# Moving the A products of a chunked delta-rule recurrence out of its per-chunk chain

## The chip, the cores and the metric

The kernel runs on one core of one Trainium2 chip. The metric is the device time of one execution in microseconds (us); lower is better. Five engines work side by side, each in the fixed order of its own instruction stream: TensorE (PE in the profile; its weight loads are PEld), VectorE (DVE), ScalarE (ACT), GpSimd (POOL), and SyncE (SP), which here only issues transfers. PSUM is the memory that PE writes its products to; SBUF holds everything else on the core.

## The reference

A decoder block over 2048 positions of 1024 channels. The input is normalised and modulated, then one projection `p = h @ w_in` feeds two branches: a causal depthwise convolution of width 31 with a layer norm, and an RWKV-7 time mixer. Both are gated, projected, merged and projected once more; the result is added to the residual and normalised. The part that matters here is the recurrence of the mixer, per head of 64 channels (16 heads):

```python
def step(state, inp):
    r_t, w_t, k_t, v_t, kk_t, b_t = inp
    sk = jnp.einsum('bhvk,bhk->bhv', state, kk_t)
    state = (state * w_t[:, :, None, :] - sk[..., None] * b_t[:, :, None, :]
             + v_t[..., None] * k_t[:, :, None, :])
    return state, jnp.einsum('bhvk,bhk->bhv', state, r_t)
```

After it, `o` gets a normalisation per head (the groupnorm below), a bonus term `r*k*v`, and the gate. All of it is in 32-bit floating point.

## The kernel before

**Tiling.** The sequence is cut into 4 blocks of 512 positions (`TB`), the 16 heads into 4 groups of 4 heads, and a group into two pairs `q`; a pair fills 128 partitions with two heads `hh`. So `group` runs 16 times. Inside a block the recurrence goes over 8 chunks `c` of 64 positions (`CH`, `NCH`). With chunks, the recurrence becomes matrix products: a 64x64 matrix per chunk and head that says how positions of the chunk act on each other, its triangular inverse, and one state `S` (per group and pair 128x128, block diagonal) that is handed from chunk to chunk.

**One group.** `pair` is a generator in three parts for each pair: it computes decays and projects and shifts k, r and v (`shifted`), fills `KR` (k and r for a chunk side by side) and `BK`, multiplies them into the matrices `As` (L513 to L531, with `BKz` as a copy of `BK` whose other head's rows are zero), puts v into its half of `uv` (L539), and transposes `BK` into `tk`. `As` of one chunk holds four 64x64 quarters: an even chunk (`e` = 0) has the inverse's quarter in partitions 64 to 127 (`prow`, `kcol`) and v in partitions 0 to 63 of `uv` (`vrow`, `rcol`); an odd chunk the other way round. Then the inverse is made: the diagonal 32x32 blocks go through memory to POOL, which inverts them by 31 steps (L589), and come back; two rounds of 32x32 products on PE (L623, L632) in the PSUM tile `late` fill the quarters between.

**The chain.** L654 to L694 go over the 8 chunks. For each one: ACT scales the state (`Se`); PE multiplies `KR` with the state into `xo` (L665); PE adds the A·v products to it, four products over 64 rows of `As` and `uv` (L670); DVE copies the x half of `xo` to `X` (L673); PE multiplies the inverse with `X` (L679); DVE scales into the other half of `uv` (L681); PE multiplies `tk` with `uv` (L685); DVE makes the new state (L690). The output of the chunk before is finished in between: `olast` adds o's A products (L650, four products over all 128 rows) to the r half of the same `xo`, and ACT copies it to `O`, which lies in `uv`. Behind the last chunk stand the groupnorm on DVE, POOL and ACT (L707 to L716), transposes of `O` on PE into `late` (L721), and the store.

**Around it.** While a chain waits, PE works on projections (`mm3`, L192): those of the convolution, of the gates, and of the next group's pairs. Each f32 value there is split in two parts, high and low, and three products are made. The convolution's 31 taps run on DVE (L756). Behind the last group, the block outputs are projected (phase 2, from L901 on), with loads through the buffers `ld` (L917) for the mixer's output of the next block (`osplit`). Phase 2's buffers on the left side of SBUF open when those of the groups close (`late.close()`, L967), so after the last group's transposes.

**What sets the order.** The program is written in the order above, and a planner with a model of the engines' times (`schedule_with_timeline_sim=True`) writes each engine's instruction stream: of what is ready in its model, what stands first in the program goes first. Each tag of a pool has a fixed number of buffers (`bufs`), and a new tile waits until a buffer is free; `late` has one PSUM bank, `aux` and `xo` two each. Between engines, semaphores do the waiting.

Of the kernel before, what the change touches and what calls it, by code (L numbers as in the profile page):

```python
# [39 lines left out]
VVT, SHT, RKT, RHT, YT = "r", "sh", "k", "sh", "y"  # L40
# [42 lines left out]
def hybrid_block(ctx: ExitStack, tc: tile.TileContext, x, vecs, convk, w2a2, final_g, ada, w_in, w_co, w_ro, w_o, crow, out,  # L83
# [359 lines left out]
    def pair(b, q_, pr, h, lora, uv, Asb, rn, res):  # L443
# [69 lines left out]
        for hh in range(2):  # L513
            hs = slice(64 * hh, 64 * hh + 64)
            nc.scalar.copy(BKz[hs, hh], BK[hs])
        for c4 in range(NCH // 4):
            for hh in range(2):
                pA = pa.tile([P, 2, 256], F32, name="aux", tag="aux")
                for c in range(4):
                    cc, e = (c4 * 4 + c) // 2, c % 2  # L520
                    es = slice(e * 128, e * 128 + 128)
                    nc.tensor.matmul(pA[:, c // 2, es], BKz[:, hh, cc, es], KR[:, cc, es],  # L522
# [35 lines left out]
    def group(b, g, h, lora, fill):  # L558
# [8 lines left out]


# [71 lines left out]
        O = uv[:, 0::2]  # L640
        Sg = S[g]
        prev = None

        def olast(c, xo):

            vr, rc = vrow(c % 2), rcol(c % 2)
            for q in range(2):
                for hh in range(2):
                    hs = slice(64 * hh, 64 * hh + 64)
                    nc.tensor.matmul(xo[vr, q, hs], As[q][:, hh, c, rc], uv[:, c, q, hs],  # L650
                                     start=False, stop=(q == 1 and hh == 1), skip_group_check=True)
            nc.scalar.copy(O[vr, c // 2], xo[vr, 0:2])  # L652

        for c in range(NCH):  # L654
            cc, e = c // 2, c % 2
            pr_, vr = prow(e), vrow(e)
# [4 lines left out]


            xo = px.tile([P, 4, P], F32, name="xo", tag="xo")
            for q in range(2):
                nc.tensor.matmul(xo[:, q, :], R[q]["KR"][:, cc, es], Sg[:, q, :], start=(q == 0), stop=False,  # L665
                                 skip_group_check=True)
            for q in range(2):
                for hh in range(2):
                    hs = slice(64 * hh, 64 * hh + 64)
                    nc.tensor.matmul(xo[pr_, q, hs], As[q][vr, hh, c, kcol(e)], uv[vr, c, q, hs],  # L670
                                     start=False, stop=False, skip_group_check=True)
            X = lt.tile([P, 2, P], F32, name="X", tag="X", bufs=1)
            nc.vector.tensor_copy(X[pr_], xo[pr_, 0:2])  # L673
            if prev:
                olast(*prev)
            for q in range(2):
                for hh in range(2):
                    hs = slice(64 * hh, 64 * hh + 64)
                    nc.tensor.matmul(xo[pr_, q, hs], As[q][pr_, hh, c, kcol(e)], X[pr_, q, hs],  # L679
                                     start=(q == 0 and hh == 0), stop=(q == 1 and hh == 1), skip_group_check=True)  # L680
# [3 lines left out]
            for q in range(2):  # L684
                nc.tensor.matmul(xo[:, 2 + q, :], R[q]["tk"][:, c, :], uv[:, c, q, :], start=False, stop=(q == 1),  # L685
                                 skip_group_check=True)
            for q in range(2):
                for hh in range(2):
                    hs = slice(64 * hh, 64 * hh + 64)
                    nc.vector.scalar_tensor_tensor(out=Sg[hs, q, hs], in0=xo[hs, 2 + q, hs],  # L690
                                                   scalar=R[q]["pe"][hs, c:c + 1], in1=Se[hs, q, hs],
                                                   op0=ALU.mult, op1=ALU.add)
            prev = (c, xo)
        olast(*prev)  # L694


# [437 lines left out]
```

## Time and profile before

| | |
|---|---|
| median of 3 runs | 3144.74 us (3140.74 to 3146.39) |
| span of the profiled execution, first to last instruction | 3131.2 us |
| mean granted TensorE clock | 0.981 |
| busy, share of the span: PE, PEld | 96%, 90% |
| busy: DVE, POOL, ACT | 69%, 36%, 33% |
| matmul instructions | 25672 |

The profile shows one execution. The median of the runs is 13.5 us above its span, for what lies before the first and after the last instruction and for the difference between runs; the profiled execution has no time of its own beside the span. Rows of the profile read: line of the code, engine, operation, output<-input, shape, count | busy us, mean ns of one | us for which the engine sat idle just before, and for what. Rows of the timeline read: start us, length us, engine, line, operation, output<-input, shape, count. A matmul of f32 values is two instructions. "Busy" joins overlapping instructions, so the sum of single durations is larger than the busy time.

### The profile page before, as it was taken

To read this page: it belongs to the slowest core of one execution; us is meant where nothing else is said; L and a number is where in the kernel's file an instruction comes from. 1 tells how busy PE (TensorE), PEld (TensorE's weight loads), DVE (VectorE), ACT (ScalarE), POOL (GpSimd) and SP (SyncE) were. 2 spreads that over 40 slices of the span, in tenths; PEclk is the share of its full clock that TensorE was granted. 3 is DMA by queue.
4 is the path that set the end of the run, shared out by engine and by line. 5 is a ranking of instruction groups with operands and counts; after the bars stand their busy time and mean duration, and the time that the engine had idled before them with its cause. 6 is when DMAs were issued, how large, how long until landed. Compare 5 with 4: busy or idle time off the path is not lost.

```text
span 3131.2 us, 64840 instructions
## 1 busy us (share of the span) xinstructions
PE 2990.4 (96%) x25672; PEld 2808.5 (90%) x25672; DVE 2169.9 (69%) x4326; ACT 1045.9 (33%) x1887; POOL 1125.1 (36%) x1692
## 2 busy tenths in 40 slices
PE   6799998999999999999999999999999999699998
PEld 5789998999999999999999999999999988487888
DVE  6686877676767665867667586758598455977643
ACT  4424333333323242423142324132332223343421
POOL 3354545424342424141313235326256014643100
PEclk9899999999999999999999999999999999899999
DMA  8665758563747476545546557636457657756554
GB/s 300 215 240 191 259 199 275 195 235 126 256 141 244 150 244 216 190 156 182 178 164 194 186 193 243 198 130 214 137 166 262 215 174 264 261 198 232 189 185 158
DMA packets 343328, 638.42 MB, mean 204 GB/s; under 512 B 133424, under 2 KB 152176, under 8 KB 343024
## 3 DMA queue, kind: packets, MB, share of 16 engines
q1 hardware_dynamic: 343024, 634.27, 60.4%
q8 instruction: 202, 3.31, 0.4%
q14 instruction: 102, 0.84, 0.1%
HBM read 462.10 MB, written 170.92 MB: 202 GB/s over the span
## 4 chain that ended last, share of the span: by engine, by line
PE 71%; DVE 10%; DMA 9%; POOL 4%; issue 2%; SPq 2%; ACT 2%; DVEq 0%; POOLq 0%; ACTq 0%
PE ps_main L192 50%; PE aux L522 3%; PE xo L679 2%; PE xo L650 2%; PE xo L670 2%; DMA w_st<-w_in_t 2%; PE xo L665 2%; PE xo L685 2%; PE pout L1055 1%; POOL TT L593 1%; PE pout L1056 1%; PE pout L1054 1%; POOL itmp L591 1%; DVE acc L756 1%; DMA w_gr<-grow_d 1%
## 5 line engine op out<-in xcount | busy, mean ns | idle before, releaser
L192 PE MATMUL ps_main<-h_hi,w_hi 128*128 128x256 f32 x4608 | 954.9, 285 | 23.1 <-ACT w_hi L175 19.7
L192 PE MATMUL ps_main<-h_hi,w_lo 128*128 128x256 f32 x4608 | 959.1, 285 | 8.1 <-POOL w_lo L177 6.6
L192 PE MATMUL ps_main<-h_lo,w_hi 128*128 128x256 f32 x4608 | 959.0, 285 | 0.0
L192 PEld LDWEIGHTS ps_main<-h_hi,w_hi 128*128 128x128 f32 x4608 | 718.8, 190 | 33.6 <-ACT w_hi L175 20.8
L192 PEld LDWEIGHTS ps_main<-h_hi,w_lo 128*128 128x128 f32 x4608 | 717.2, 189 | 17.9 <-POOL w_lo L177 8.2
L192 PEld LDWEIGHTS ps_main<-h_lo,w_hi 128*128 128x128 f32 x4608 | 717.7, 189 | 6.8 <-issue 0.5
L756 DVE SCALAR_TENSOR_TENSOR acc<-u,ck,acc 128x512 f32<-128x512 f32 x928 | 697.9, 752 | 20.4
L175 ACT CAST w_hi<-w_st 128x1024 fp32r<-128x1024 f32 x135 | 141.5, 1048 | 327.7 <-DMA w_st<-w_in_t 120.8
L591 POOL TENSOR_TENSOR itmp<-La,TT 128x126 f32<-128x126 f32 (+22 forms) x496 | 179.8, 363 | 137.4 <-DMA La<-dA 102.1
L690 DVE SCALAR_TENSOR_TENSOR S<-xo,pe,Se 64x64 f32<-64x64 f32 x512 | 144.8, 283 | 108.4 <-PE xo L685 99.1
L593 POOL TENSOR_TENSOR TT<-TT,itmp 128x126 f32<-128x126 f32 (+22 forms) x496 | 191.9, 387 | 36.0
L177 DVE TENSOR_TENSOR w_lo<-w_st,w_hi 128x1024 fp32r<-128x1024 f32 x88 | 117.8, 1339 | 110.0 <-PE ps_main L192 53.7
L660 ACT ACTIVATE Se<-S,pe 128x128 f32<-128x128 f32 x256 | 89.1, 394 | 232.7 <-DVE S L690 232.3
L177 POOL TENSOR_TENSOR w_lo<-w_st,w_hi 128x1024 fp32r<-128x1024 f32 x47 | 112.5, 2394 | 136.2 <-ACT w_hi L175 83.5
L545 POOL TENSOR_TENSOR vv<-rk,vv 128x512 f32<-128x512 f32 x32 | 43.2, 1350 | 324.4 <-ACT rk L544 324.4
L681 DVE TENSOR_TENSOR uv<-xo,rn 64x256 f32<-64x256 f32 x128 | 53.9, 421 | 129.7 <-PE xo L679 128.7
L522 PE MATMUL aux<-KR,BKz 128*128 128x128 f32 x1024 | 139.9, 282 | 2.8 <-DVE As L524 2.1
L522 PEld LDWEIGHTS aux<-KR,BKz 128*128 128x128 f32 x1024 | 126.2, 194 | 5.7 <-DVE As L524 2.4
L524 DVE TENSOR_TENSOR As<-aux,maskA 128x512 f32<-128x512 f32 x128 | 86.8, 687 | 52.8 <-PE aux L522 51.9
L673 DVE COPY X<-xo 64x256 f32<-64x256 f32 x128 | 53.6, 419 | 89.5 <-PE xo L670 88.6
L652 ACT COPY uv<-xo 64x256 f32<-64x256 f32 x128 | 46.8, 365 | 175.7 <-PE xo L650 175.2
L665 PE MATMUL xo<-S,KR 128*128 128x128 f32 x512 | 96.4, 280 | 6.9 <-DVE S L690 6.7
(294 smaller groups left out, 5464.1 us busy)
## 6 DMA issues: line engine op xcount, KB each, us to landing
w_hi<-kh_in SPq DMA_DIRECT2D x219, 512.0 KB, 3.8
w_lo<-kl_in SPq DMA_DIRECT2D x219, 512.0 KB, 4.9
w_st<-w_in_t SPq DMA_DIRECT2D x73, 512.0 KB, 4.4
kh_in<-w_hi SPq DMA_DIRECT2D x71, 512.0 KB, 2.9
kl_in<-w_lo SPq DMA_DIRECT2D x71, 512.0 KB, 4.3
w_st<-w_ro_t SPq DMA_DIRECT2D x32, 512.0 KB, 3.9
w_st<-w_co_t SPq DMA_DIRECT2D x32, 512.0 KB, 3.5
w_hi<-kh_o SPq DMA_DIRECT2D x32, 512.0 KB, 3.6
```

The source lines that it names most:

```text
L175: nc.scalar.copy(hi, st)
L177: lo_eng.tensor_tensor(out=lo, in0=st, in1=hi.bitcast(F32), op=ALU.subtract)
L192: nc.tensor.matmul(ps[:, qs], ww[:, k, :], aa[k][:, qs], start=(k == 0 and t == 0 and q == 0), stop=(k == KT - 1 and t == 2 and q == ms - ...
L522: nc.tensor.matmul(pA[:, c // 2, es], BKz[:, hh, cc, es], KR[:, cc, es], start=(c == 0), stop=(c == 3), skip_group_check=True)
L524: nc.vector.tensor_tensor(out=Asb[:, hh, c4 * 4:c4 * 4 + 4, :].rearrange("p (a e) n -> p a (e n)", e=2), in0=pA, in1=flat(maskA).unsqueeze ...
L591: nc.gpsimd.tensor_tensor(out=tmp[:, :ni, :nt], in0=La[:, j:j + 1, j + 1:].broadcast_to([P, ni, nt]), in1=TT[:, :ni, j:j + 1].broadcast_to ...
L593: nc.gpsimd.tensor_tensor(out=TT[:, :ni, j + 1:], in0=TT[:, :ni, j + 1:], in1=tmp[:, :ni, :nt], op=ALU.add)
L650: nc.tensor.matmul(xo[vr, q, hs], As[q][:, hh, c, rc], uv[:, c, q, hs], start=False, stop=(q == 1 and hh == 1), skip_group_check=True)
L660: nc.scalar.mul(Se[:, q, :], Sg[:, q, :], R[q]["pe"][:, c:c + 1])
L665: nc.tensor.matmul(xo[:, q, :], R[q]["KR"][:, cc, es], Sg[:, q, :], start=(q == 0), stop=False, skip_group_check=True)
L690: nc.vector.scalar_tensor_tensor(out=Sg[hs, q, hs], in0=xo[hs, 2 + q, hs], scalar=R[q]["pe"][hs, c:c + 1], in1=Se[hs, q, hs], op0=ALU.mult ...
L756: nc.vector.scalar_tensor_tensor(out=acc if i + 1 < HALO else yj, in0=u[:, i:i + TB], scalar=ck[:, j, i:i + 1], in1=acc, op0=ALU.mult, op1 ...
```

## The change

- **A·v ahead of the inverse.** A new tile `XO` (8 chunks, both pairs, 128 partitions, one buffer) is set to zero in the `vrow` rows by POOL, two memsets a group. For four chunks at a time, sixteen A·v products (the same as L670's) go into one PSUM tile of the tag `aux`, and ACT copies it to `XO`, two copies each time.
- **The chain.** L670, the copy to `X` and `olast` go. DVE adds `XO[:, c]` to both halves of `xo` in place, over 128 partitions; the inverse's products read `XO`.
- **o behind the last state.** For four chunks at a time, o's sixteen A products go into one PSUM tile of the tag `late`. They are held behind the last of the chain's `tk` products in PE's stream (`issue_after`). DVE adds them into `XO`, two adds each time, and `O` now is a view of `XO`.
- **Room for XO.** `BKz` holds four chunks, not eight, and is filled twice (ACT, four half copies a pair for two whole ones); `y` shares the buffer of `M`, `s_lo` that of `sq`; `ld` in phase 2 has five buffers for six.

```diff
-VVT, SHT, RKT, RHT, YT = "r", "sh", "k", "sh", "y"
+VVT, SHT, RKT, RHT, YT = "r", "sh", "k", "sh", "M"
...
-        lo = e1.tile([P, TB], F32R, name="s_lo", tag="s_lo")
+        lo = e1.tile([P, TB], F32R, name="s_lo", tag="sq")
...
-    BKz = c1.tile([P, 2, NCH // 2, 4 * CH], F32, name="BKz")
+    BKz = c1.tile([P, 2, NCH // 4, 4 * CH], F32, name="BKz")
...
-        for hh in range(2):
-            hs = slice(64 * hh, 64 * hh + 64)
-            nc.scalar.copy(BKz[hs, hh], BK[hs])
         for c4 in range(NCH // 4):
+            for hh in range(2):
+                hs = slice(64 * hh, 64 * hh + 64)
+                nc.scalar.copy(BKz[hs, hh], BK[hs, c4 * 2:c4 * 2 + 2])
...
+        XO = lt.tile([P, NCH, 2, P], F32, name="XO", tag="XO", bufs=1)
+        for e in range(2):
+            nc.gpsimd.memset(XO[vrow(e), e::2], 0.0)
+        heads = [(q, hh) for q in range(2) for hh in range(2)]
+        for c4 in range(NCH // 4):
+            pv = pa.tile([P, 2, 2, P], F32, name="aux", tag="aux")
+            for c in range(4 * c4, 4 * c4 + 4):
+                e = c % 2
+                for q, hh in heads:
+                    hs = slice(64 * hh, 64 * hh + 64)
+                    nc.tensor.matmul(pv[prow(e), c // 2 % 2, q, hs], As[q][vrow(e), hh, c, kcol(e)], uv[vrow(e), c, q, hs],
...
+            for e in range(2):
+                nc.scalar.copy(XO[prow(e), 4 * c4 + e:4 * c4 + 4:2], pv[prow(e)])
...
-            for q in range(2):
-                for hh in range(2):
-                    hs = slice(64 * hh, 64 * hh + 64)
-                    nc.tensor.matmul(xo[pr_, q, hs], As[q][vr, hh, c, kcol(e)], uv[vr, c, q, hs],
-                                     start=False, stop=False, skip_group_check=True)
-            X = lt.tile([P, 2, P], F32, name="X", tag="X", bufs=1)
-            nc.vector.tensor_copy(X[pr_], xo[pr_, 0:2])
-            if prev:
-                olast(*prev)
...
+            nc.vector.tensor_tensor(out=XO[:, c], in0=xo[:, 0:2], in1=XO[:, c], op=ALU.add)
...
+        O = XO[:, 0::2]
+        for c4 in range(NCH // 4):
+            po = pl.tile([P, 2, 2, P], F32, name="late", tag="late")
+            with tc.issue_after(last.ins if hasattr(last, "ins") else last):
+                for c in range(4 * c4, 4 * c4 + 4):
+                    e = c % 2
+                    for q, hh in heads:
+                        hs = slice(64 * hh, 64 * hh + 64)
+                        nc.tensor.matmul(po[vrow(e), c // 2 % 2, q, hs], As[q][:, hh, c, rcol(e)], uv[:, c, q, hs],
...
+            for e in range(2):
+                sl = slice(4 * c4 + e, 4 * c4 + 4, 2)
+                nc.vector.tensor_tensor(out=O[vrow(e), 2 * c4:2 * c4 + 2], in0=po[vrow(e)], in1=XO[vrow(e), sl], op=ALU.add)
...
-        t_ = ob.tile([P, TB], F32, name=name, tag="ld", bufs=6)
+        t_ = ob.tile([P, TB], F32, name=name, tag="ld", bufs=5)
```

More of the change, by code (lines that the diff above doesn't have):

```diff
@@ L521, in pair @@
                     es = slice(e * 128, e * 128 + 128)
-                    nc.tensor.matmul(pA[:, c // 2, es], BKz[:, hh, cc, es], KR[:, cc, es],
+                    nc.tensor.matmul(pA[:, c // 2, es], BKz[:, hh, c // 2, es], KR[:, cc, es],
                                      start=(c == 0), stop=(c == 3), skip_group_check=True)
@@ L637, in group @@
                 nc.vector.tensor_copy(As[q][lo_, :, e::2, hi_], pq[lo_, q])
[L640 removed]
         Sg = S[g]
[L642 to L652 removed]
         for c in range(NCH):
             cc, e = c // 2, c % 2
[L656 removed]
+            pr_ = prow(e)
             es = slice(e * 128, e * 128 + 128)
```

35 lines of the change are left out of this document (16 added, 19 removed).

## The prediction

> **What bounds the kernel now.** I read the page's busy times first, then stretches of the span, then the groups of TensorE instructions with their shapes apart, then the order of TensorE's instructions around one chunk. The busy times:
>
> ```profile
> span 3131.2 us, 64840 instructions
> PE 2990.4 (96%) x25672; PEld 2808.5 (90%) x25672; DVE 2169.9 (69%) x4326; ACT 1045.9 (33%) x1887; POOL 1125.1 (36%) x1692
> ```
>
> The same by stretch (start:end, length, then busy PE, PEld, DVE, ACT, POOL, the granted clock, the DMA share, GB/s):
>
> ```profile
> 210.00:2490.00 2280.00, 2246.93 (x21089) 2160.57 (x21089) 1626.37 (x3314) 753.70 (x1375) 863.31 (x1455) 0.99 0.60 198
> 2490.00:2590.00 100.00, 99.48 (x531) 80.13 (x530) 53.45 (x84) 29.69 (x48) 14.59 (x10) 0.97 0.57 193
> 2640.00:2760.00 120.00, 89.53 (x396) 69.52 (x395) 106.30 (x153) 49.22 (x80) 86.61 (x56) 0.89 0.69 236
> ```
>
> The span of all state updates (L690), and that of one group's inverse products (L679), in the view of single lines:
>
> ```profile
> L690 DVE SCALAR_TENSOR_TENSOR S<-xo,pe,Se x512: 248/285/294, 209.2 to 2583.1; 64x64 f32<-64x64 f32 x171
> ```
> ```profile
> L679 PE MATMUL xo<-X,As x64: 218/218/268, 983.1 to 1068.2; 64*64 64x64 f32 x64
> ```
>
> So all chains of state lie between 210 and 2590. There PE is busy 2346 of 2380 us (98.6%), and its clock is granted almost whole. So a shorter dependency gains nothing there by itself; only time that PE spends less does. What the chain's own matmuls cost PE, and how little PE idles for them (last column):
>
> ```profile
> L665 PE MATMUL xo<-S,KR 128*128 128x128 f32 x512 | 96.4, 280 | 6.9 <-DVE S L690 6.7
> L679 PE MATMUL xo<-X,As 64*64 64x64 f32 x1024 | 89.6, 226 | 3.0 <-DVE X L673 1.8 <-DVE As L637 1.1
> L650 PE MATMUL xo<-uv,As 128*64 128x64 f32 x1024 | 88.2, 230 | 0.0
> L670 PE MATMUL xo<-uv,As 64*64 64x64 f32 x1024 | 87.8, 226 | 0.0
> L685 PE MATMUL xo<-uv,tk 128*128 128x128 f32 x512 | 79.2, 277 | 3.6 <-DVE uv L681 3.6
> ```
>
> All five together cost 13.5 us of idle PE in the whole run. Each f32 matmul is two instructions, so x1024 is 16 groups of 8 chunks of 4 products.
>
> **What a piece of small matmuls costs PE.** PE's order around one chunk, around a lone piece of eight, around one that the order tears in two, and around a long run of tiny ones:
>
> ```profile
> 991.04 0.38 PE L665 MATMUL xo<-S,KR 128*128 128x128 f32 x2
> 991.17 0.48 PE L192 MATMUL ps_main<-h_hi,w_hi 128*128 128x256 f32 x2
> 991.49 0.38 PE L665 MATMUL xo<-S,KR 128*128 128x128 f32 x2
> 991.80 0.68 PE L670 MATMUL xo<-uv,As 64*64 64x64 f32 x8
> 992.41 0.68 PE L650 MATMUL xo<-uv,As 128*64 128x64 f32 x8
> 993.02 0.50 PE L192 MATMUL ps_main<-h_lo,w_hi 128*128 128x256 f32 x2
> 993.36 0.40 PE L192 MATMUL ps_main<-h_hi,w_lo 128*128 128x256 f32 x2
> ```
> ```profile
> 1031.38 0.40 PE L192 MATMUL ps_main<-h_hi,w_hi 128*128 128x256 f32 x2
> ...
> 1031.85 0.28 PE L192 MATMUL ps_main<-h_hi,w_lo 128*128 128x256 f32 x1
> 1032.06 0.68 PE L679 MATMUL xo<-X,As 64*64 64x64 f32 x8
> 1032.67 0.39 PE L192 MATMUL ps_main<-h_hi,w_lo 128*128 128x256 f32 x1
> 1032.89 0.40 PE L192 MATMUL ps_main<-h_hi,w_hi 128*128 128x256 f32 x2
> ```
> ```profile
> 983.06 0.44 PE L679 MATMUL xo<-X,As 64*64 64x64 f32 x4
> 983.43 0.39 PE L192 MATMUL ps_main<-h_hi,w_lo 128*128 128x256 f32 x1
> 983.75 0.44 PE L679 MATMUL xo<-X,As 64*64 64x64 f32 x4
> ```
> ```profile
> 971.34 2.11 PE L623 MATMUL late<-T,As 32*32 32x32 f32 x64
> 973.37 0.50 PE L192 MATMUL ps_main<-h_lo,w_hi 128*128 128x256 f32 x2
> ```
>
> A projection matmul takes 0.1175 us (1031.38 to 1031.85 for four). A lone piece of eight: 1031.85 to 1032.89 is 1.04 us, less the two projection matmuls in it 0.805. Eight take 0.68 where four take 0.44, so one more matmul inside a piece is 0.06, and going into and out of such a piece costs 0.805 - 8 x 0.06 = 0.325 us beside the matmuls. L665 pays no such thing: 991.04 to 991.49 is 0.45 for two of it and two projection matmuls, so 0.215 for two.
>
> **The change, part by part.** *Out of the chain:* L670 and L650 leave each chunk. 991.49 to 993.36 is 1.87 us; less two L665 (0.215) and two projection matmuls (0.235) they cost 1.42 us per chunk, over 128 chunks 181.8 us of PE.
>
> *Into bursts:* the same products come back, 32 instructions a burst, two bursts of A·v ahead of the inverse and two of o behind the last state in each of 16 groups: 64 bursts. Whole, a burst costs 0.805 + 24 x 0.06 = 2.245 us, together 143.7. So PE gains 38.1 us. Two things are not shown. First, a burst passes from one chunk's 64x64 place in the array to the next one's, three times. Nearest is L623: its 64 matmuls sit in two places and take 2.03 us with way in and out, 0.032 each, so the change of place is nearly nothing; the other end is the whole 0.325, 3 x 64 x 0.325 = 62 us, which would make it 24 us slower. I take nothing, by L623. The Trainium skill, "TensorEngine Tiling (Array Packing)", Key Properties, says that a change of tiling mode drains the engine and a change of tile within a mode does not; by that rule the sum is the 38.1, and the 0.325 around each piece agrees with it. Second, the order may tear a burst. 983.06 to 983.75 shows why a piece gets torn: pair 0's operand was there before pair 1's. A·v has the same two operands, o behind the last state has not. I take one tear in each A·v burst, 32 x 0.325 = 10.4 us; bounds none and the rival below. PE: -27.7 us.
>
> *DVE, ACT, POOL.* The durations:
>
> ```profile
> L673 DVE COPY X<-xo 64x256 f32<-64x256 f32 x128 | 53.6, 419 | 89.5 <-PE xo L670 88.6
> L1062 DVE TENSOR_TENSOR xt<-pout,xt 128x256 f32<-128x256 f32 x64 | 24.2, 417 | 71.9 <-PE pout L1056 71.7
> L524 DVE TENSOR_TENSOR As<-aux,maskA 128x512 f32<-128x512 f32 x128 | 86.8, 687 | 52.8 <-PE aux L522 51.9
> L539 ACT COPY uv<-aux 64x512 f32<-64x512 f32 x64 | 37.1, 580 | 86.7 <-PE aux L537 86.3
> L515 ACT COPY BKz<-BK 64x1024 f32<-64x1024 f32 x64 | 67.0, 1046 | 42.2 <-POOL BK L503 39.0 <-DVE r L422 2.5
> L275 POOL MEMSET BKz<- 64x1024 f32 x1 | 0.9, 950 | 0.1
> L756 DVE SCALAR_TENSOR_TENSOR acc<-u,ck,acc 128x512 f32<-128x512 f32 x928 | 697.9, 752 | 20.4
> ```
>
> The copy X becomes an add over 128x256: nearest is L1062, 417 against 419 ns, nothing. Four o adds a group are new, 64 x 0.687 = 44 us of DVE (69% to 71%), hidden under PE's projections. ACT loses one o copy a chunk and takes 64 copies like L539, 37 us; the half copies of BKz, like L539 too, are 128 x 0.58 = 74 for 67.0. POOL gets two memsets a group, 32 x 0.95 = 30 us, at 36% busy. None of the three sets the end here; uncovered, the four adds would cost 2.7 us a group, 44 us.
>
> *Waits that are new.* The halved BKz makes the second four chunks' copies wait for the first four's L522; L522 is 128 by 128 as L665 is, so it needs no way in or out, and PE has projections to put between. XO has one buffer, so a group's memsets wait for the transposes (L721) of the group before. By the order of the code that is no later than the chain waits already: the inverse's bank `late` is behind the same transposes. Behind the memset on POOL stand tail copies and the inverse's products; behind the A·v copies on ACT, the evacuations of projections. `y` in M's slot and `s_lo` in `sq`'s follow the order in which the pairs run anyway. I cost these at nothing; the cover is PE's backlog, and without it the price is rival two's.
>
> *The last stage.* Five `ld` buffers for six. In 2640 to 2760 PE waits, DVE is busy 106 of 120 us and the loads feed POOL and DVE:
>
> ```profile
> L192 PE MATMUL ps_main<-m_hi,w_lo 128*128 128x512 f32 x64 | 28.3, 443 | 17.4 <-DVE w_lo L177 17.0 <-DVE rs L125 0.3
> L926 POOL TENSOR_TENSOR ot<-ot,bt 128x512 f32<-128x512 f32 x14 | 22.6, 1618 | 12.8 <-DMA bt<-bv_d 10.2 <-DVE cth L943 2.4 <-DVE rs_t L128 0.2
> L927 POOL TENSOR_TENSOR ot<-ot,rt 128x512 f32<-128x512 f32 x14 | 22.1, 1584 | 11.7 <-DMA rt<-ro_d 11.6
> ```
>
> POOL's 21.8 us of waits for loads grow by a sixth to a fifth, 4 us, most of it on the way to PE: +3, bounds 0 and 5. The issues of these loads sit in SP's one queue ahead of weights, which is why I don't take 0.
>
> **Sum.** -27.7 + 3 is -25 us on the span of 3131.2, so 3106. The median of the runs shown, 3144.74, lies 13.5 us above that span (what lies around the first and last instruction, and the spread between runs); I leave that as it is: 3120 us.
>
> **Rivals.** *One: no change, about 3144.* The series of chains, not PE, sets when the last group ends, and PE's saving comes back as idle. For it: one chain's inverse products run from 983.1 to 1068.2, 85 us of the 149 that a group has on average (2380 / 16), and behind it come o, the groupnorm, the transposes and the inverse's two products in `late`, in one row. The bursts add 2 x 2.245 us and four adds (2.7) to that row, 7 us, about what 8 chunks without L670 (8 x 0.6 us) give back. Against it: PE idles only 33 us in the 2280. Also here: the order puts the products back among the chunks, so that the change does little. Chance 0.13.
>
> *Two: slower through `late`, about 3152.* `late` has one bank, now with two more tenants a group. The second o burst can't start before two adds (1.4 us) that stand behind a running convolution tap (0.75, L756); if PE's fixed order has it next, PE stands 2.1 us a group, 34 us: -25 + 34 = +9. It decides from 1.6 us a group on. Against it: L721 takes turns in the same bank today. Chance 0.07.
>
> *Three: slower through torn bursts, about 3170.* The pairs are made one after the other, so A·v products are ready for pair 0 before pair 1, and each that is put alone between projections pays 0.325. From 3.7 extra pieces per A·v burst (38.1 / (32 x 0.325)) the gain is gone; in eight pieces it is 7 x 32 x 0.325 = 72.8, so -38 + 73 + 3 = +38, and with the o bursts whole I call it +25 to +38. For it: the torn L679. Against it: most pieces in the rows above are whole. Chance 0.09.
>
> **How the numbers follow.** The forecast has the remaining 0.71. Its own range: from whole bursts, no loss at the end and the chain's 13.5 us of idle gone (-38.1 - 13.5, 3093) to about -7 (3138). For 8 in 10 I reach through rival one to rival two: 3093 to 3152. About 0.2% (6.3 us) is what a measurement of this kernel can tell from no change. Faster by more: 0.71; within it, rival one, 0.13; slower, rivals two and three, 0.16.
>
> **What would show it.** Right: L192's runs unbroken where L670 and L650 stood; the A·v and o groups near 64 pieces with about 0.06 us a matmul; PE's busy time in the chain stage down some 25 to 40 us with idle as before; projections ending that much earlier. Wrong: many pieces of two or four among projections (rival three); idle of PE ahead of the o group put down to its DVE adds (rival two); PE's busy time down and its idle up as much, with the last L721 where it was (rival one). A longer stage after the last group, with waits for `ot`, `bt`, `rt`, would say that the fifth buffer weighed more than 3 us.

## The result and the profile after

The changed kernel takes 3104.40 us (median of 4 runs, 3104.17 to 3109.53) against 3142.74 (3137.01 to 3146.39) for the kernel before, run beside it: a ratio of 0.9884, with a 95% interval of 0.9869 to 0.9898. That is 38 us, or 1.2%, faster. A second series of the same kernel gave 3103.43, ratio 0.9874 [0.9840, 0.9909]. Every interval below is a 95% interval against the kernel before in the same series, whose medians there were 3140.8, 3139.6 and 3138.4; a difference between two experiments is one of medians and can hold some 5 us of chance.

The spans of the two profiled executions, 3131.2 and 3102.4 us, differ by 28.8 us, less than the medians. The changed kernel's profiled execution took 3104.22 us, so 1.8 us lies around its span. With the same 1.8 the profiled execution of before took 3133, below all of its four runs here: most of the 13.5 us that the prediction put around the span was difference between executions.

The page of the changed kernel, busy times:

```profile
span 3102.4 us, 65048 instructions
PE 2934.1 (95%) x25672; PEld 2776.6 (89%) x25672; DVE 2205.1 (71%) x4390; ACT 1042.7 (34%) x1887; POOL 1153.6 (37%) x1724
```

The same stretches that the prediction showed of before (columns as there):

```profile
210.00:2490.00 2280.00, 2210.44 (x21254) 2140.99 (x21255) 1681.80 (x3419) 757.95 (x1387) 890.60 (x1484) 0.98 0.61 199
2490.00:2590.00 100.00, 89.27 (x453) 71.72 (x452) 69.60 (x92) 30.42 (x43) 35.41 (x22) 0.96 0.68 234
2640.00:2760.00 120.00, 98.64 (x375) 75.15 (x376) 99.38 (x164) 46.30 (x69) 60.71 (x39) 0.91 0.72 240
```

The groups of the chain, shapes apart (busy us, mean ns | PE's idle time before them, and for what). L579 is the A·v burst, L693 the o burst; L671 is L679 of before, L677 is L685, L666 is L665:

```profile
L522 PE MATMUL aux<-KR,BKz 128*128 128x128 f32 x1024 | 141.9, 286 | 7.8 <-ACT BKz L516 4.8 <-DVE As L524 2.3 <-ACT ta L460 0.6
L666 PE MATMUL xo<-S,KR 128*128 128x128 f32 x512 | 95.6, 281 | 10.4 <-DVE S L681 10.0
L671 PE MATMUL xo<-XO,As 64*64 64x64 f32 x1024 | 89.8, 226 | 9.2 <-DVE XO L668 5.1 <-DVE As L653 4.1
L677 PE MATMUL xo<-uv,tk 128*128 128x128 f32 x512 | 80.4, 280 | 8.6 <-DVE uv L673 8.6
L693 PE MATMUL late<-uv,As 128*64 128x64 f32 x1024 | 50.0, 230 | 5.4 <-DVE XO L698 5.4
L579 PE MATMUL aux<-uv,As 64*64 64x64 f32 x1024 | 48.1, 227 | 0.3 <-ACT tk L554 0.3
L490 PE MATMUL aux<-bones,sq 128*64 128x2 f32 x512 | 23.4, 206 | 10.1 <-ACT sq L486 10.1
L724 PE MATMUL late<-ident,XO 128*128 128x128 f32 x128 | 19.4, 274 | 4.4 <-POOL XO L719 4.4
```

Two things are to be seen. The moved products, as many as before and each as long as before (227 and 230 ns), took 88.2 + 87.8 = 176.0 us of PE's busy time in the chain and take 48.1 + 50.0 = 98.1 in the bursts: 78 us less, where the prediction forecast 38. And PE waits more: 33 us of idle in the first stretch (2280 - 2246.93) became 70 (2280 - 2210.44) although the work fell, and the chain's groups that stood at 13.5 us together now stand at 28.2 (10.4 + 9.2 + 8.6). Beside them stand L693's 5.4 us, and L522 and L490, which before had these rows:

```profile
L522 PE MATMUL aux<-KR,BKz 128*128 128x128 f32 x1024 | 139.9, 282 | 2.8 <-DVE As L524 2.1 <-ACT BKz L515 0.8
L490 PE MATMUL aux<-bones,sq 128*64 128x2 f32 x512 | 21.5, 200 | 0.7 <-ACT sq L486 0.5 <-ACT M L455 0.2
```

**Work and waits kept apart.** Busy time alone hides part of this, since PE's busy time is longer where the granted clock is 0.50. For each kernel I summed PE's busy time that lies in stretches with that clock, and call half of it lost, as if it would be half as long at the full clock. Work is busy time less that half; idle is span less busy. The three add up to the span.

| kernel | span | PE's work | idle | lost at half clock | idle + lost |
|---|---|---|---|---|---|
| before | 3131.2 | 2947 | 141 | 43 | 184 |
| changed | 3102.4 | 2861 | 168 | 73 | 241 |
| difference | -28.8 | -86 | +27 | +30 | +57 |

The mean clocks agree with it: (1 - 0.981) x 3131.2 is 59 us and (1 - 0.970) x 3102.4 is 93, which also count idle time under the low clock. So the change took 86 us of work off PE and gave 57 back in waits and in the lower clock. The prediction had -28 and 0.

Three things limit how exactly this can be read. A projection matmul at half the clock took 0.43 us for 0.235 (rows further down), 1.8 times and not 2; with that the last difference would be -83 and +54. The profiled execution of before was about 10 us quicker than the median of its runs, so about 10 of the 57 may be chance. And in one experiment below, the room alone, the work differs by 7 us although PE makes the same products.

### The profile page after: what moved, and what is told of

Read it like the earlier page. It is cut to its first block, busy times and chain, and to the rows that moved or that the text cites. A ratio compares the mean times of both kernels' runs of the same rounds, so it can differ in the third digit from the quotient of the medians.

```text
span 3102.4 us, 65048 instructions
## 1 busy us (share of the span) xinstructions
PE 2934.1 (95%) x25672; PEld 2776.6 (89%) x25672; DVE 2205.1 (71%) x4390; ACT 1042.7 (34%) x1887; POOL 1153.6 (37%) x1724
## 4 chain that ended last, share of the span: by engine, by line
PE 63%; DVE 11%; DMA 11%; POOL 7%; issue 4%; ACT 3%; SPq 2%; DVEq 0%; POOLq 0%; ACTq 0%
PE ps_main L192 44%; PE aux L522 3%; DMA w_st<-w_in_t 2%; POOL TT L609 2%; POOL itmp L607 2%; PE xo L671 2%; PE pout L1057 2%; PE pout L1058 2%; PE pout L1059 2%; DMA w_gr<-grow_d 2%; PE xo L666 1%; PE xo L677 1%; DVE acc L759 1%; DVE M L463 1%; SPq L620 1%
## 5 line engine op out<-in xcount | busy, mean ns | idle before, releaser
L522 PE MATMUL aux<-KR,BKz 128*128 128x128 f32 x1024 | 141.9, 286 | 7.8 <-ACT BKz L516 4.8
L522 PEld LDWEIGHTS aux<-KR,BKz 128*128 128x128 f32 x1024 | 130.4, 201 | 10.3 <-ACT BKz L516 5.5
L739 ACT ACTIVATE th<-ps_main 128x512 f32<-128x512 f32 x64 | 38.2, 596 | 211.4 <-PE ps_main L192 159.4
L666 PE MATMUL xo<-S,KR 128*128 128x128 f32 x512 | 95.6, 281 | 10.4 <-DVE S L681 10.0
L771 ACT ACTIVATE th<-ps_main 128x512 f32<-128x512 f32 x64 | 38.2, 597 | 183.3 <-PE ps_main L192 178.5
```

The costliest lines, as they stand in the source:

```text
L522: nc.tensor.matmul(pA[:, c // 2, es], BKz[:, hh, c // 2, es], KR[:, cc, es], start=(c == 0), stop=(c == 3), skip_group_check=True)
```

## The experiments

In the table the last three columns are worked out of each one's profiled execution as above; the differences are against the changed kernel. (The room alone, in brackets, is an edit of the kernel before.) The profiled executions of the bursts by turns (3079.71 us) and of the o bursts alone (3175.78) are the fastest and the slowest of four, 12 us below and 7 above their medians, so their last two columns are off by about as much.

| experiment | median, us | ratio to before | work | idle + lost | span |
|---|---|---|---|---|---|
| changed kernel again | 3103.43 | 0.9874 [0.9840, 0.9909] | +1 | -1 | +1 |
| A·v bursts alone | 3135.99 | 0.9989 [0.9975, 1.0003] | +61 | -30 | +31 |
| o bursts alone | 3168.93 | 1.0087 [1.0066, 1.0109] | +59 | +13 | +72 |
| bursts by place | 3115.38 | 0.9916 [0.9896, 0.9935] | +22 | -8 | +14 |
| bursts by turns | 3091.64 | 0.9841 [0.9822, 0.9861] | -14 | -11 | -25 |
| the room alone | 3144.98 | 1.0011 [0.9996, 1.0025] | (+93) | (-48) | (+45) |
| longer chain | 3152.18 | 1.0036 [1.0018, 1.0053] | +2 | +50 | +52 |
| o not held back | 3122.57 | 0.9944 [0.9926, 0.9961] | +55 | -31 | +24 |
| inverse by turns | 3078.71 | 0.9798 [0.9762, 0.9833] | -22 | -1 | -23 |
| all by turns | 3068.91 | 0.9766 [0.9743, 0.9789] | -46 | +8 | -38 |
| A·v made twice | 3111.78 | 0.9907 [0.9879, 0.9936] | +43 | -35 | +8 |
| o bursts in `aux` | 3701.37 | 1.1786 [1.1752, 1.1819] | -10 | +605 | +595 |

### What a change of place in the array costs

The bursts of the changed kernel, from PE's order behind the last state of group 5 (start, us, engine, line, count):

```profile
1063.83 0.60 PE L677 MATMUL xo<-uv,tk 128*128 128x128 f32 x4
1064.37 1.54 PE L693 MATMUL late<-uv,As 128*64 128x64 f32 x32
1065.84 0.39 PE L192 MATMUL ps_main<-h_hi,w_lo 128*128 128x256 f32 x1
...
1066.62 2.57 PE L579 MATMUL aux<-uv,As 64*64 64x64 f32 x62
1069.12 1.54 PE L693 MATMUL late<-uv,As 128*64 128x64 f32 x32
1070.60 0.33 PE L579 MATMUL aux<-uv,As 64*64 64x64 f32 x2
```

A product's place is the part of PE's array that it uses, given by the partitions of its operands and its output. The counts are matmul instructions, two to a product. A whole o burst of 32 takes 1.47 us (1064.37 to 1065.84) where the prediction had 2.245, and 62 of a group's 64 A·v instructions take 2.50 (1066.62 to 1069.12). The chunks of a burst alternate between two places, so the place changes every eight instructions. In the trace's single records, instructions of these pieces start 58 ns apart within a place; around each change of place some start 4 to 6 ns after the one before: the next place's products overlap the last ones of this place. To test that, the same products were put in two other orders.

**By place:** both bursts do their even chunks and then their odd ones, so that the place changes once.

```diff
-            for c in range(4 * c4, 4 * c4 + 4):
+            for c in (4 * c4, 4 * c4 + 2, 4 * c4 + 1, 4 * c4 + 3):
```

> The change, but within each burst the even chunks first and then the odd ones, so that the place in the array changes once in 32 instructions instead of three times. Theory (matmuls of neighbouring places overlap where the place changes, which is why a burst's matmul takes 0.039 and 0.043 us and not 0.058): about two thirds of that overlap goes, some 20 us more PE time, 8 to 20 us slower than the change. Rival (a change of place costs time or nothing): the same as the change within 3 us, or faster.

**By turns:** an even and an odd chunk take turns product by product, so that the place changes at every product.

```diff
+        def turns(c4):
+            return [(4 * c4 + 2 * a + e, q, hh) for a in range(2) for q, hh in heads for e in range(2)]
...
-            for c in range(4 * c4, 4 * c4 + 4):
-                e = c % 2
-                for q, hh in heads:
+            for c, q, hh in turns(c4):
+                    e = c % 2
...
```

> The change, but within each burst even and odd chunks by turns, product by product. Theory (overlap of neighbouring places): down to about 0.03 us a matmul, 64 x 0.010 + 64 x 0.013 us a group, 23 us less PE time over 16 groups, 8 to 23 us faster than the change. Rival (a change of place costs something, up to the 0.325 of a way in and out): 31 changes a burst instead of 3, slower by 5 us or more; with no effect of place, no difference.

PE's timeline, by place:

```profile
1068.51 1.90 PE L693 MATMUL late<-uv,As 128*64 128x64 f32 x32
...
1071.13 3.29 PE L579 MATMUL aux<-uv,As 64*64 64x64 f32 x62
```

By turns:

```profile
1042.90 1.15 PE L695 MATMUL late<-uv,As 128*64 128x64 f32 x32
...
1044.77 2.07 PE L582 MATMUL aux<-uv,As 64*64 64x64 f32 x62
```

The same 62 instructions take 3.29, 2.57 and 2.07 us as the place changes once in a burst of 32, every eight and at every product, and the 32 of o 1.90, 1.54 and 1.15. The times follow: 3115.4, 3104.4, 3091.6, that is 11 us more and 13 less than the changed kernel, both within what was expected. By place the work rose 22 us, by turns it fell 14 (20 and 23 had been expected). So a change of place is a gain here. The Trainium skill, "TensorEngine Tiling (Array Packing)", Key Properties, also states that different tiles can load weights and multiply in parallel; these rows agree, and show that it needs the places to alternate in the program's order.

### The same on the inverse's products

The inverse's two products run in 32x32 places, all of one place and then all of the other. **Inverse by turns** takes the changed kernel and lets the two places alternate; **all by turns** does that and the bursts by turns.

```diff
-        for e in range(2):
-            lo_, hi_ = quarters(e)
-            for n, (q, hh, c) in enumerate(every):
+        for n, (q, hh, c) in enumerate(every):
+            for e in range(2):
+                lo_, hi_ = quarters(e)
...
```

> The change with the two rounds of 32x32 products alone by turns of their two places, bursts as in the change. Theory (neighbouring places overlap; the gains add): 29 us less PE work, of which part comes back as waiting, 10 to 25 us faster than the change. Rival (the fastest version's gain needs the bursts by turns, or is the planner's order): within 6 us of the change.

> Bursts by turns as in the run by turns, and the two rounds of 32x32 products that finish the inverse by turns of their two places too. Theory (neighbouring places overlap): 64 products from 2.0 us to about 1.1, two rounds, 16 groups, 29 us less PE time, 10 to 29 us faster than the run by turns. Rival (the gain of the run by turns was the planner's order): no faster than that run.

The changed kernel's piece of 64, and the same piece by turns:

```profile
962.38 2.11 PE L639 MATMUL late<-T,As 32*32 32x32 f32 x64
```
```profile
1123.05 1.20 PE L639 MATMUL late<-T,As 32*32 32x32 f32 x64
1128.04 1.20 PE L648 MATMUL late<-As,Qs 32*32 32x32 f32 x64
```

0.033 us an instruction (2.11 / 64) became 0.019 (1.20 / 64). These two loops were no part of the change, and turning them round brings 25 us; with both, 3068.91 us is 35 us below the changed kernel and 71 below the kernel before in the same series, the best time of all. Both gains lie within what was expected. The page of all by turns:

```profile
span 3064.5 us, 65076 instructions
PE 2880.9 (94%) x25672; PEld 2720.8 (89%) x25672; DVE 2202.3 (72%) x4390; ACT 1040.4 (34%) x1887; POOL 1160.7 (38%) x1724
```

Against the changed kernel PE's busy time fell 53 us and the span 38; in work it is 46, of which only 8 came back as idle and lost time. Most of the saving shows in the time.

That need not be because PE has less to do. The inverse's two rounds stand in a sequence that each group runs through alone: inverse, chain, o, groupnorm, transposes, and then the next group's inverse, which starts 3 to 16 us behind those transposes in 12 of the 15 cases, in the changed kernel as well as with the inverse by turns. From the first product of the inverse to its last, the 16 groups take 141 us in the changed kernel and 111 with the inverse by turns. So the 25 us can be this shorter sequence as well as PE's 22 us of work, and the same holds for o's bursts by turns; no run tells the two apart for these products. Two experiments further down, one that lengthens the sequence with no more work for PE and one that adds work beside it, show which counts for more in the changed kernel.

### Either half alone

**A·v bursts alone:** o's products go back into the chain, where they stood, and with them their copies. **o bursts alone:** the A·v products go back into the chain, and XO receives the copy from `xo`. POOL's memsets of XO go in both.

```diff
-        for c4 in range(NCH // 4):
-            po = pl.tile([P, 2, 2, P], F32, name="late", tag="late")
...
-            nc.vector.tensor_tensor(out=XO[:, c], in0=xo[:, 0:2], in1=XO[:, c], op=ALU.add)
+            nc.vector.tensor_tensor(out=XO[pr_, c], in0=xo[pr_, 0:2], in1=XO[pr_, c], op=ALU.add)
+            if prev:
+                olast(*prev)
```

> A·v ahead of the inverse as in the change; o's A products back in the chain, one piece of eight a chunk with its copy on ACT. Theory (PE time: what counts is how many times PE goes into and out of small pieces, and how cheap a matmul is in a burst): a chunk's 1.42 us for both kinds becomes one lone piece of 0.805, 79 us less in 128 chunks, and the A·v bursts, 2.8 us a group in the changed kernel's trace, cost 45 us: 34 of the 84 us of PE work that the whole change saves by the same reckoning, so about 0.4 of the measured gain, 15 us faster than before. Rival (a shorter chain sets the pace): A·v was on the way from state to state and o was not, so nearly all of the gain, 30 us or more.

```diff
-        for c4 in range(NCH // 4):
-            pv = pa.tile([P, 2, 2, P], F32, name="aux", tag="aux")
...
-            nc.vector.tensor_tensor(out=XO[:, c], in0=xo[:, 0:2], in1=XO[:, c], op=ALU.add)
...
+            for q, hh in heads:
+                hs = slice(64 * hh, 64 * hh + 64)
+                nc.tensor.matmul(xo[pr_, q, hs], As[q][vrow(e), hh, c, kcol(e)], uv[vrow(e), c, q, hs],
+                                 start=False, stop=(q == 1 and hh == 1), skip_group_check=True)
+            nc.vector.tensor_copy(XO[:, c], xo[:, 0:2])
```

> o behind the last state as in the change; A·v products back in the chain, behind the state's products. Theory (PE time): 79 us less for the chunks, 53 us for the o bursts (3.3 us a group), so 26 of the 84 us, about 0.3 of the measured gain, 12 us faster than before. Rival (a shorter chain): o's products were never on the way from state to state, so no gain, within 6 us of before.

A·v alone gains 5 us or nothing (3135.99), o alone loses 28 (3168.93); the two together gain 38. All that was expected of the halves fell: the theory's gains of 15 and 12 us, the rival's 30 us and more with A·v alone, and its "within 6 us" with o alone. In work each half saves only 24 to 27 us of the 86. The prediction's rows agree with that: in the chain of before the two pieces stand side by side (991.80 and 992.41), so they share one way in and out, and taking one of them out saves 0.61 us a chunk, 78 us, of which its own 32 bursts take back 47 at 1.47 us each: some 31 are left, and 24 and 27 were measured. By this reckoning the way in and out, the rest of the 1.42 us a chunk, goes only when both are gone; that is worked out from the rows and fits the two measured sums, and no run tests it by itself. The waits differ as well: against before, 27 us more with A·v alone and 70 more with o alone. The page of o alone:

```profile
PE 2994.0 (94%) x25672; PEld 2813.4 (89%) x25672; DVE 2236.7 (70%) x4390; ACT 1006.1 (32%) x1823; POOL 1125.9 (35%) x1692
```

PE is as busy as before (2990.4) over a span 43 us longer (3174.1). Of its idle time 21.1 us stand before L522 (2.8 before), 12.4 for ACT's BKz and one wait of 8.1 for an instruction of the convolution on DVE. Why the waits are so much larger there than with A·v alone was not settled.

### Where the 57 us of waits come from

**The room alone:** the kernel before, with the half `BKz`, `y` in M's buffer, `s_lo` in that of `sq`, and five `ld` buffers, and nothing moved.

```diff
-VVT, SHT, RKT, RHT, YT = "r", "sh", "k", "sh", "y"
+VVT, SHT, RKT, RHT, YT = "r", "sh", "k", "sh", "M"
-        lo = e1.tile([P, TB], F32R, name="s_lo", tag="s_lo")
+        lo = e1.tile([P, TB], F32R, name="s_lo", tag="sq")
...
-    BKz = c1.tile([P, 2, NCH // 2, 4 * CH], F32, name="BKz")
+    BKz = c1.tile([P, 2, NCH // 4, 4 * CH], F32, name="BKz")
...
-        t_ = ob.tile([P, TB], F32, name=name, tag="ld", bufs=6)
+        t_ = ob.tile([P, TB], F32, name=name, tag="ld", bufs=5)
```

> The kernel before with the change's edits for room alone: BKz for four chunks filled twice, y in M's buffer, s_lo in sq's, five ld buffers; chain, A·v and o as before. Theory (these edits cost PE waits, and each wait is followed by a stretch at half clock; that is why the halves of the change gained 5 and lost 28 us where PE work fell by 34 and 26): 10 to 25 us slower than before. Rival (as predicted: 0 to 5 us): within 6 us of before, and the halves' losses came from the order that the planner found for them.

1.0011 [0.9996, 1.0025], so between 1 us faster and 8 slower: after the result I had thought of 10 to 25 us here, and that fell. Idle and lost time are 193 against 184 us before. The prediction's +3 (0 to 5) can stand, though one wait that it put at nothing shows: PE stands 6.0 us before L522 for BKz, 0.8 before.

**A longer chain:** the changed kernel with one more copy in each chunk's chain, on ACT, behind the add to XO. It computes nothing new.

```diff
             nc.vector.tensor_tensor(out=XO[:, c], in0=xo[:, 0:2], in1=XO[:, c], op=ALU.add)
+            nc.scalar.copy(XO[:, c], XO[:, c])
```

> The change with one more step in each chunk: ACT copies XO's chunk onto itself between DVE's add and the inverse's products (128 x 256, some 0.4 us and a hand-over each way, 0.6 us and more on the way from state to state, 5 us and more a group), no more PE work. Theory (PE's time sets the pace and projections fill the chain's waits): within 10 us of the change. Rival (the chain's length sets the pace): 16 times 5, so 60 to 90 us slower than the change.

```profile
PE 2951.9 (94%) x25672; PEld 2786.1 (88%) x25672; DVE 2222.9 (70%) x4390; ACT 1088.5 (35%) x2015; POOL 1155.4 (37%) x1724
...
L672 PE MATMUL xo<-XO,As 64*64 64x64 f32 x1024 | 90.3, 228 | 16.7 <-ACT XO L669 10.9 <-DVE As L653 5.8
```

The 128 copies are busy 51.6 us, 0.40 us each (ACT's busy time grew by 45.8 in all), and the kernel grew by 48. PE has no more work (+2 us), but 50 us more of idle and lost time; PE alone stands 16.7 us for the inverse's products, 9.2 without the copies. The theory of at most 10 us fell, and the rival's 60 to 90, which counted the hand-overs as well, was not reached. In the changed kernel the length of the copies is paid for nearly one for one, though PE is 95% busy.

How a short wait can cost more than its length, in the changed kernel, PE's timeline with the idle time before a piece in brackets:

```profile
300.50 0.40 PE L192 MATMUL ps_main<-h_hi,w_lo 128*128 128x256 f32 x2
302.76 0.67 PE L671 MATMUL xo<-XO,As 64*64 64x64 f32 x8 [1.86 <-DVE XO L668]
303.36 0.51 PE L192 MATMUL ps_main<-h_hi,w_hi 128*128 128x256 f32 x2
...
304.42 0.46 PE L192 MATMUL ps_main<-h_lo,w_hi 128*128 128x256 f32 x2
304.67 0.63 PE L192 MATMUL ps_main<-h_hi,w_lo 128*128 128x256 f32 x2
305.10 0.63 PE L192 MATMUL ps_main<-h_hi,w_hi 128*128 128x256 f32 x2
```

and the stretches around it (granted clock is the third column from the end):

```profile
299.00:300.90 1.90, 1.90 (x17) 1.69 (x15) 0.41 (x1) 1.50 (x3) 1.59 (x5) 1.00 0.11 44
300.90:304.60 3.70, 1.84 (x18) 1.78 (x19) 3.63 (x6) 0.63 (x2) 3.23 (x7) 1.00 0.81 239
304.60:308.00 3.40, 3.40 (x18) 3.40 (x18) 3.23 (x6) 1.54 (x2) 2.61 (x5) 0.50 0.81 327
```

PE stands 1.86 us for XO; from 304.6 on the clock is 0.50 for 3.4 us, and two projection matmuls take 0.43 us (304.67 to 305.10) where they took 0.235. The wait costs 1.86 us and the stretch behind it about 1.5 more (3.4 less 3.4 x 0.235 / 0.43).

Such stretches do not all stand behind waits. The changed kernel's trace has 31 of them, that of before 19. Three of the 31, at 215.9, 372.9 and 700.6 us, start when PE has been idle for only 0.06, 0.49 and 0.28 us of the 3.4 us before; about 2 of these 3.4 us are the inverse's 32x32 products (1.96, 2.11 and 2.01). One of before, at 2326.2, starts with no idle time at all, behind 2.11 us of such products. So what is called lost here is in part not the price of a wait. One wait of L490 shows what stands in front of it, on POOL, ACT and PE of the changed kernel (idle time before the instruction in brackets):

```profile
988.72 1.26 POOL L156 TENSOR_TENSOR w_st<-w_st,w_gr 128x512 f32<-128x512 f32 x1 [4.47 <-DMA w_gr<-grow_d]
```
```profile
990.01 0.62 ACT L157 CAST w_hi<-w_st 128x512 fp32r<-128x512 f32 x1 [5.51 <-POOL w_st L156]
990.54 0.72 ACT L486 ACTIVATE sq<-k,v 128x512 f32<-128x512 f32 x1
```
```profile
991.31 0.92 PE L490 MATMUL aux<-bones,sq 128*64 128x2 f32 x14 [3.13 <-ACT sq L486]
```

POOL waits for a weight's row to be loaded, ACT's conversion of that weight (L157) waits for POOL, `sq` stands behind it in ACT's queue, and PE waits 3.13 us for `sq`. None of these instructions was edited, and POOL waited for this load before too (60.4 us in 15 places, 55.7 in 14 now). That they meet in this order here is what the planner wrote for the changed program; it was not tried by itself.

**A·v made twice:** the A·v burst's loop runs over its chunks two times, which gives PE some 40 us more work ahead of the inverse and writes the same values again. The A·v bursts run beside the groupnorm of the group before (1066.62 above, with that group's transposes at 1093), so they stand beside the sequence that the longer chain lengthened, but for o's second burst, which passes PE behind them.

```diff
-            for c in range(4 * c4, 4 * c4 + 4):
+            for c in 2 * list(range(4 * c4, 4 * c4 + 4)):
```

> The change with each A·v product made twice, the second time over the first: 32 more products a group, about 2.5 us, 40 us more PE work in all, with no other dependency. Theory (PE work counts, but what is saved of it partly comes back as waiting): 20 to 40 us slower than the change. Rival (the chain's length sets the pace, PE has room): within 6 us of the change.

```profile
PE 2962.8 (95%) x26696; PEld 2804.6 (90%) x26696; DVE 2204.8 (71%) x4390; ACT 1042.7 (34%) x1887; POOL 1150.7 (37%) x1724
```

1024 more matmul instructions and 43 us more work cost 8 us; idle and lost time fell by 35. So at this place about four fifths of added work goes where PE would have stood. The expected 20 to 40 fell, and the rival's 6 was missed by 2. Together with the longer chain this says that in the changed kernel a microsecond of the sequence counts for more than a microsecond of PE's work beside it.

### The order behind the last state

**o not held back:** the o products may go as soon as their chunk's operand is there.

```diff
-            with tc.issue_after(last.ins if hasattr(last, "ins") else last):
+            if True:
```

> The change without the hold behind the last state: the planner may put o's A products where it likes. Theory (ways in and out of small pieces count, 0.325 us each): o's products come chunk by chunk, up to six more pieces a group, 96 x 0.325 = 31 us of PE time, less overlap of places, 10 to 40 us slower than the change. Rival: o's bursts stay whole because the rest of PE's work stands first in the program, no difference within 6 us.

```profile
988.36 0.68 PE L671 MATMUL xo<-XO,As 64*64 64x64 f32 x8
...
991.89 0.60 PE L677 MATMUL xo<-uv,tk 128*128 128x128 f32 x4
992.43 0.68 PE L693 MATMUL late<-uv,As 128*64 128x64 f32 x8
```

The o products come in 143 pieces, mostly of eight, for 32 whole ones: work +55 us, idle and lost time -31, time +19, within the theory's 10 to 40. So the price of pieces, on which rival three rests, is real, and holding the bursts back is what kept it away from o.

**o bursts in `aux`:** everything by turns, with the o bursts' PSUM tile from `aux` (two banks), not from `late`.

```diff
-            po = pl.tile([P, 2, 2, P], F32, name="late", tag="late")
+            po = pa.tile([P, 2, 2, P], F32, name="aux", tag="aux")
```

> The fastest version so far (all by turns) with o's two bursts in the two buffers of aux and not in the one of late. Theory (the waits for late are few, 4.6 us in that version's trace, and a wait costs about as much again at half clock): 0 to 10 us faster than that version. Rival (late holds up the row from the last state to the next chain): 15 us faster or more. Against both: aux is the pairs' bank too, and the pairs may now wait.

Theory and rival fell, and the doubt beside them, that the pairs may wait, held: 3701 us, 600 more. PE's busy tenths in 40 slices, and its order behind one group's last state:

```profile
PE   6878888887979797979797979797975798889998
```
```profile
1220.97 3.22 PE L695 MATMUL aux<-uv,As 128*64 128x64 f32 x64
1224.53 0.47 PE L452 MATMUL aux<-lw,wl 128*128 128x512 f32 x1 [0.34 <-DVE XO L700]
```

The next group's pairs (L452 first) start only behind the o bursts, in all 15 cases; in the changed kernel group 6's L522 runs while the chain of group 5 still goes (1003.3 to 1036.7, chain to 1064). Chain and pairs then take turns, and idle and lost time come to 846 us. The likely reason is that buffers of one tag are handed out in the program's order, and the o bursts stand ahead of the next pairs there; the order is shown, this reason is argued.

## Why the prediction came out right, step by step

The time, 3104.4, lies in the range (3093 to 3152) and on the forecast side, 16 us below the 3120. Its sum on the span was -25 and -28.8 was measured, but out of two terms that were both wrong and offset each other: -86 us of work for -28, and +57 of idle and lost time for 0. That the sum came so near is luck; the way of the change was not.

*PE bounds the kernel; a shorter dependency gains nothing.* Half right: PE's work is a limit, and not the only one. It fell 86 us and the span only 29. Copies of 52 us in the chain cost 48, and 43 us of work beside it cost 8, so in the changed kernel the chain is paid for first. Whether that held for the kernel before was not run; its 13.5 us of idle in the chain's groups was read as proof that it didn't, and that is more than the row shows.

*Out of the chain, 181.8 us.* Either half alone saves 24 to 27 us of work, which agrees with a shared way in and out, the 1.42 us of the prediction. The sum holds, as far as these rows can show it.

*Into bursts, 143.7 us; a change of place costs nothing.* This is the term that was mis-sized. A whole burst measured 1.47 us, not 2.245, and the moved products' busy time fell by 78 us. The range from 0 to 0.325 us for a change of place left out a gain, although the row taken for it, L623 with 0.032 us an instruction in two places, lay far below the 0.06 of an instruction within a piece. The two experiments on the order show the gain: 22 us of work lost with fewer changes, 14 won with more.

*One tear in each A·v burst, 10.4 us.* Wrong, by little: with its tears 64 pieces of A·v were assumed, and the trace has 29 in 16 groups, since both bursts of a group run on into each other, as the 62 + 2 above.

*DVE, ACT, POOL hidden.* DVE's busy time rose 35 us (44 forecast), POOL's 28 (30), ACT's fell 3. The four adds show on PE in L693's 5.4 us, which wait for them, and they lengthen the way from the chain to the transposes (below).

*New waits cost nothing; the cover is PE's backlog.* Wrong in sum, +57 us of idle and lost time, though only a little of it by the waits that were named: the wait of L522 for the halved BKz grew from 0.8 to 4.8 us. The room alone costs 3 to 5 us by medians, within -1 to +8. What grew was waits for the chain (L666, L671, L677: 13.5 to 28.2 us), L490 behind ACT's queue (0.7 before, 10.1 after), L693 (5.4), and the time lost at half clock (30 us), part of it behind these waits. That PE has less work to put into the chain's gaps is a likely reason; A·v made twice, where 35 us of idle and lost time went when work was added, agrees with it.

*Last stage, +3.* In 2640 to 2760 PE is 98.6 us busy for 89.5; from the first `pout` product to the end it took 520 us for 530 (2582.5 and 2601.3 to the ends of the spans). But counted from the last transposes it took 541 for 516: of the 54 us by which they come earlier (next paragraph), 25 do not reach the end. With the room alone it took 516 too, so five `ld` buffers by themselves do not explain it; what does was not tested.

*Rival one, the chain sets the pace.* It lost as a forecast: the last transposes (L721, now L724) come at 2561.0 for 2614.8, 54 us earlier, and the last projection of h at 2466.8 for 2486.7:

```profile
L721 PE MATMUL late<-ident,uv x128: 270/272/328, 326.6 to 2614.8; 128*128 128x128 f32 x128
L724 PE MATMUL late<-ident,XO x128: 270/272/328, 352.1 to 2561.0; 128*128 128x128 f32 x128
```

Its sequence is there all the same. Summed over the 16 groups, the time from the inverse's last product to the last state's `tk` product fell from 1540 to 1447 us, 5.8 us a group, and the time from there to the last transpose grew from 499 to 553, 3.4 us a group; the rival had 4.8 and 7. *Rival two, `late`:* L693 waits 5.4 us for its adds, at three places and not in all 16 groups, for the 34 us of the rival; PE has projections and the next group's A·v to put between the two o bursts (1065.84 to 1069.12 above). *Rival three, torn bursts:* no burst fell into small pieces here (the 29 pieces of A·v are mostly 62 and 2, or 48 and 16), and it cost 19 us when o's bursts are not held back. By its own +9 on 3144.74 the time of rival two, and with it the upper end of the range, is 3154 and not 3152; the result is far from both.

What stays open: which of the waits come from the chain's length and which from the order that the planner wrote, since every edit changes both; and how much of the 38 us came from PE's work and how much from the shorter chain, since the change gives both at once.

## What to carry to other kernels

Let small products alternate between places of the array in program order: it costs a reordered loop, and here it gave 35 us on the bursts and the inverse, nearly as much as the whole change's 38. When a chain and a full engine share the time, count work, idle and clock loss apart in both profiles, and expect part of the work saved to come back as waits; ask of each product whether it stands in the sequence that each group must run through, or beside it. If the row taken for one end of a range shows less per product than the sum itself counts, the range must allow a gain as well.

## What had not been expected of the hardware

- Products of two places overlap: 0.053 us an instruction when the place changes once in 32 (3.29 / 62), 0.041 every eight (2.57 / 62), 0.033 at every product (2.07 / 62); for 32x32 products from 0.033 (2.11 / 64) to 0.019 (1.20 / 64).
- A wait of 1.86 us was followed by 3.4 us at half the clock. The Trainium skill, "TensorE: Matmul & The Clock Gate", "Why this matters for your kernels", advises against gaps of more than about 3 us; here the row shows that a shorter one can be enough. Of the changed kernel's 21 waits of PE of 1.8 us and more outside such stretches, 19 run into one or have one start within 3.5 us of their end, and two (1.84 and 2.14 us) do not. All 31 stretches start on one grid of 3.41 us, so where a wait falls may decide; that was not tested. In the whole run PE was busy for 145 us at half the clock, against 86 before, and some of these stretches follow small products and no wait (above).
